# Small products of the tensor engine ordered as lists, and shape changes priced in the ordering model of a two-block kernel

## The chip, the cores and the metric

The kernel runs on one core of a Trainium2 chip. The metric is the device time of one execution in microseconds (us), and the median of several runs is given. The engines are named as in the profile: PE is the tensor engine, PEld its weight loads, DVE the vector engine, ACT the scalar engine, POOL the GpSimd engine and SP the engine that issues most transfers.

## The reference

Two transformer blocks follow each other, on one sequence of 256 positions and width 1024, all in fp32. Cut to what matters here:

```python
# first block: three mixers, a gate, a feed-forward net
proj = rms_norm(x, g_mix) @ w_in           # q_mla, c_kv, k_rope, q_gla, k_gla, v_gla, ..., gates
o_mla = causal_block_attention(q_full, k_full, v_mla, ...)    # 8 heads of 128 + 64 (rotary)
# a[i,j] = sum_d q[i,d] k[j,d] exp(b[i,d] - b[j,d]), in chunks of 64, 4 heads of 128
og = gla_chunked(qg, kg, vg, log_a)
s_m = einsum('bshd,bmhd->bhsm', q_m, k_m) * MEM_DQK ** -0.5    # 4 heads of 64, 256 memory rows
x = x + (gates * [o_mla, o_gla, o_mem]).sum() @ w_o
x = x + square(relu(rms_norm(x, g_ffn) @ w_up)) @ w_down

# second block: a state space branch and a dilated attention
u_s, z_s, q, k, v, z_a, r_s, r_a = split(rms_norm_2(x, norm_w) @ w_in)
y_s = s5_branch(u_s, ...)     # 64 groups of 16 channels, 64 complex states: h = a h + B u, y = Re(C h) + D u
y_a = dilated_attention(q, k, v)   # 8 heads of 64; window 128 at step 1, 512 at step 4, 2048 at step 16
x = x + (sigmoid(r_s) * (y_s * silu(z_s)) @ w_ssm_out + sigmoid(r_a) * (y_a * silu(z_a)) @ w_attn_out) @ w_o
```

## The kernel before

Nothing in the kernel is issued where it is written. The methods of `Net` (one for each stage: `gla_scores`, `mem_attn`, `mla_attn`, `ssm_quarter`, `ssm_scan`, `heads`, `values`, `dilated` and others) call engines through a `Recorder`, and `Plan.add` notes each call as an operation with its buffers and its dependences. `Plan.latest` gives each operation a priority, by a list schedule that runs backwards from the end. `Plan.order` then runs forwards: it keeps a clock for each engine, takes the operation that can start first, by priority among those that are ready, and adds the operation's price (`Plan.price`, in ns) to that engine's clock. An operation gets its buffer when it is taken, from a pool with a fixed number of slots, `BUFS`: 5 of `wr` (weights as they arrive), 4 each of `wh` and `wl` (their high and low parts), 26 of `k4`, 11 of `k2` and 24 of `sm` (results and small vectors), 8 of `ps` (PSUM banks). `Plan.emit` issues the operations in the order found. So each engine's queue is fixed when the program is built, by the prices; on the chip each engine works its queue off in that order and waits wherever an input is not there. All instructions have the line of the emission, L535.

The large products take fp32 weights in two parts: ACT casts `wr` to `wh`, DVE subtracts `wl <- wr, wh`, and PE makes three products for each pair of tiles. They carry some 90% of PE's time.

The change is about the small products, plain fp32, each of which takes two passes of PE in the trace:

- `gla_scores`: per level of the chunked decay 8 products of 64 or 4 x 8 products of 32 rows and columns, then a masked copy on DVE.
- `mem_attn`: 2 pairs of heads; a product is 64 rows (one head's width, on partitions 0 to 63 or 64 to 127) by 128 columns by 256.
- `mla_attn`: for a pair of heads 4 products over 128 rows, and 4 over the 64 rotary rows, which lie on opposite partition halves for the two heads.
- `ssm_quarter`: 16 products of 64 x 32, for each of four quarters of the state space's channels.
- `ssm_scan`: per quarter X = G U, 16 products of 64 x 64 for the real and as many for the imaginary part; ACT copies X out of PSUM, DVE and POOL run the scan to H; then y = T U + C H, 16 products and 32.
- `dilated`: for a pair of heads b and a tile tt of 128 queries, a score tile per head: one product of 64 rows x 128 columns x 256 ("own", the group with step 1) and four of 64 x 64 ("near", the other groups). `softmax_rows` is a masked reduction on DVE, an exponential on ACT and a scaling on DVE; PE transposes, ACT copies, then 12 products of 128 rows x 64 columns make the outputs.

Each of these is an operation of its own in the plan, so that `order` may put a matrix product of another stage, or a transpose, between any two. The price does not depend on what came before on PE. Between 545 and 645 us the scan runs beside `heads` (products, norms and transposes of queries and keys) and before `values`.

## Time and profile before

| | |
|---|---|
| runs | 875.13, 876.12, 878.0 us (median 876.12) |
| profiled execution | 874.69 us, span from first to last instruction 872.8 us |
| mean granted PE clock | 0.996 |
| busy: PE, PEld, DVE, ACT, POOL | 853.1, 757.7, 631.4, 477.4, 22.6 us |
| DMA | 142.09 MB, mean 163 GB/s |

Times count from the start of the span. A row of the timeline joins instructions that follow each other and are alike; its second number is the time from the first one's start to the last one's end, and since PE's products overlap, the start of the next row, not this end, says when PE went on. "64*128 64x256" is a product of 64 rows by 128 columns of weights with 256 moving columns, and "x4" counts passes. The clock is a share of 2.4 GHz.

### The profile page before, as it was taken

The numbers are of one execution on the slowest core, as the hardware profiler recorded it, in microseconds if no ns is written. First come the engines' busy times: TensorE is split into PE (matmuls) and PEld (weight loads), VectorE is DVE, ScalarE is ACT, GpSimd is POOL, SyncE is SP. The second block draws the span as 40 slices with busy tenths as digits, with TensorE's granted clock in tenths as the row PEclk, the third lists the DMA queues.
The fourth block names the chain that finished last, engine by engine and source line by source line (L and its number), as shares of the span: only waits on it lengthen the run. The fifth ranks groups of instructions, "written<-read, shape, count | busy, mean of one in ns | idle before, by whom it ended". The sixth has DMA issues, their size and how long they took to land.

```text
span 872.8 us, 16700 instructions
## 1 busy us (share of the span) xinstructions
PE 853.1 (98%) x6572; PEld 757.7 (87%) x6572; DVE 631.4 (72%) x1478; ACT 477.4 (55%) x782; POOL 22.6 (3%) x40
## 2 busy tenths in 40 slices
PE   8999899999999999999999989999999999999998
PEld 6998787789999989999999878877779769999996
DVE  6998998896756679945544956949997665653584
ACT  6756867644445567555555574444456563554352
POOL 1000000000000000000000051010000000000000
PEclk9999999999999999999999999999999999999999
DMA  9775442145355665665655546661245413565551
GB/s 326 245 238 160 130 126 72 49 137 182 118 192 187 184 210 190 186 192 183 187 183 187 190 125 215 189 210 50 97 135 172 129 50 116 177 192 191 173 177 63
DMA packets 42638, 142.09 MB, mean 163 GB/s; under 512 B 5888, under 2 KB 7040, under 8 KB 42560
## 3 DMA queue, kind: packets, MB, share of 16 engines
q1 hardware_dynamic: 40944, 137.39, 49.4%
q0 software_dynamic: 1472, 3.61, 1.4%
q8 instruction: 51, 0.84, 0.4%
q14 instruction: 27, 0.22, 0.1%
q10 hardware_dynamic: 144, 0.04, 0.0%
HBM read 138.46 MB, written 2.56 MB: 162 GB/s over the span
## 4 chain that ended last, share of the span: by engine, by line
PE 86%; DVE 7%; ACT 3%; issue 2%; DMA 1%; SPq 0%; DVEq 0%; POOL 0%; ACTq 0%; POOLq 0%
PE ps L535 86%; DVE k L535 5%; ACT k L535 2%; DVE sm L535 1%; DVE wl L535 1%; ACT wh L535 1%; DMA wr<-w_mv 1%; DMA k<-ud 1%; SPq L535 0%; DVE c L535 0%; ACT L535 0%; ACT c L535 0%; DVEq L1804 0%; POOL ud L535 0%; ACTq L535 0%
## 5 line engine op out<-in xcount | busy, mean ns | idle before, releaser
L535 DVE TENSOR_TENSOR wl<-wr,wh 128x1024 fp32r<-128x1024 f32 (+2 forms) x258 | 301.7, 1191 | 162.2 <-ACT wh L535 159.5
L535 ACT CAST wh<-wr 128x1024 fp32r<-128x1024 f32 (+2 forms) x258 | 257.5, 1024 | 231.7 <-PE ps L535 205.0
L535 PE MATMUL ps<-k,wh 128*128 128x256 f32 x2048 | 371.8, 284 | 0.5 <-DVE k L535 0.5
L535 PEld LDWEIGHTS ps<-k,wh 128*128 128x128 f32 x2048 | 320.4, 192 | 3.1 <-issue 1.0
L535 PE MATMUL ps<-wh,k 128*128 128x512 f32 (+2 forms) x1024 | 314.0, 384 | 1.7 <-ACT wh L535 1.4
L535 PE MATMUL ps<-k,wl 128*128 128x256 f32 x1024 | 289.6, 283 | 0.6 <-DVE wl L535 0.6
L535 PEld LDWEIGHTS ps<-wh,k 128*128 128x128 f32 x1024 | 188.8, 188 | 38.4 <-ACT wh L535 2.8
L535 PE MATMUL ps<-wl,k 128*128 128x512 f32 (+2 forms) x512 | 196.8, 385 | 2.3 <-DVE wl L535 2.1
L535 PEld LDWEIGHTS ps<-k,wl 128*128 128x128 f32 x1024 | 196.3, 192 | 1.6 <-DVE wl L535 1.0
L535 PEld LDWEIGHTS ps<-wl,k 128*128 128x128 f32 x512 | 96.4, 188 | 22.3 <-DVE wl L535 5.0
L535 DVE TENSOR_TENSOR k<-k,k 128x512 f32<-128x512 f32 (+8 forms) x192 | 91.7, 499 | 13.5 <-ACT k L535 12.9
L535 PE MATMUL ps<-k,k 64*64 64x64 f32 (+7 forms) x1224 | 85.7, 256 | 2.7 <-ACT k L535 2.2
L535 PEld LDWEIGHTS ps<-k,k 64*64 64x64 f32 (+5 forms) x1224 | 62.3, 142 | 23.7 <-issue 13.5
L535 ACT ACTIVATE k<-ps 128x512 f32<-128x512 f32 (+2 forms) x86 | 44.8, 534 | 54.7 <-PE ps L535 54.6
L535 ACT COPY k<-ps 128x512 f32<-128x512 f32 (+7 forms) x119 | 50.7, 456 | 35.1 <-PE ps L535 34.1
L535 PE MATMUL ps<-c,k 128*128 128x128 f32 (+3 forms) x344 | 57.0, 296 | 7.2 <-DVE k L535 3.9
L535 ACT ACTIVATE k<-k 128x512 f32<-128x512 f32 (+3 forms) x72 | 46.5, 672 | 27.2 <-DVE k L535 25.1
L535 PEld LDWEIGHTS ps<-c,k 128*128 128x128 f32 (+2 forms) x344 | 40.8, 149 | 19.6 <-ACT k L535 7.1
L535 DVE TENSOR_TENSOR k<-k,c 128x64 f32<-128x64 f32 (+7 forms) x176 | 47.7, 317 | 0.1
L535 ACT ACTIVATE k<-ps,c 128x256 f32<-128x256 f32 (+2 forms) x76 | 37.0, 540 | 16.3 <-PE ps L535 16.3
L535 DVE SCALAR_TENSOR_TENSOR k<-k,k 128x256 fp32r<-128x256 f32 (+4 forms) x61 | 32.7, 569 | 11.7 <-ACT k L535 11.4
L535 DVE CUSTOM_DVE_ANT_0 k<-ps,c 128x384 f32<-128x384 f32 (+2 forms) x32 | 14.4, 455 | 10.3 <-PE ps L535 10.2
(74 smaller groups left out, 323.4 us busy)
## 6 DMA issues: line engine op xcount, KB each, us to landing
wr<-w_up SPq DMA_DIRECT2D x32, 512.0 KB, 3.9
wr<-w_down SPq DMA_DIRECT2D x32, 512.0 KB, 4.2
wr<-w_gt SPq DMA_DIRECT2D x24, 512.0 KB, 4.0
wr<-w_o SPq DMA_DIRECT2D x16, 512.0 KB, 4.0
wr<-w_k SPq DMA_DIRECT2D x12, 512.0 KB, 4.0
wr<-w_q SPq DMA_DIRECT2D x12, 512.0 KB, 4.1
wr<-w_v SPq DMA_DIRECT2D x12, 512.0 KB, 4.3
wr<-w_qkg SPq DMA_DIRECT2D x8, 512.0 KB, 3.9
```

Of the source, the lines that this page charges most:

```text
L535: getattr(getattr(tc.nc, op.eng), op.name)(*map(live, op.args), **{k: live(v) for k, v in op.kw.items()})
```

## The change

- A new PE operation, `products`, holds a list of products. It is ordered, priced and emitted as one piece; its dependences are those of all its members. Used for: each level of `gla_scores`, the scores of a pair of heads in `mem_attn`, `mla_attn` (over 128 rows first, then rotary) and `dilated` (both own, then near), the 16 products of `ssm_quarter`, in `ssm_scan` X's real part, X's imaginary part, the U products of y and the H products of y, and the 12 products of a `dilated` output. Within the lists for pairs of heads, the two heads alternate.
- `Plan.tiling` gives a product's tile: rows and columns rounded up to 32, 64 or 128. Where it differs from that of the PE operation before, `order` starts the operation later by `SWITCH` = 90 ns plus columns / 1.2, and so it does inside a list.
- Three prices change: 32 columns and over 32 moving 30 to 38 ns; 128 rows x 64 x 64 from 142 to 112; 128 rows, up to 64 columns, more moving columns: 1.15 ns for each.

The products themselves are the same, 5742 PE instructions before and after; the emission of a list has the line L564 and that of other operations L566. The diff, cut to its core:

```diff
+SWITCH = 90
@@ -197,8 +199,12 @@
-        views = [a for a in (*args, *kw.values()) if isinstance(a, View)]
-        outs = [kw["out"]] if "out" in kw else [args[0]]
+        if name == "products":
+            views = [v for a, _ in args[0] for v in a]
+            outs = [a[0] for a, _ in args[0]]
+        else:
+            views = [a for a in (*args, *kw.values()) if isinstance(a, View)]
+            outs = [kw["out"]] if "out" in kw else [args[0]]
@@ -214,6 +220,7 @@
+        op.mode = tuple(self.tiling(*(args[0][j][0] if name == "products" else args)) for j in (0, -1)) if eng == PE else None
@@ -282,9 +289,24 @@
-    def price(op):
+    def tiling(out, l, r):
+        part = lambda n: 32 if n <= 32 else 64 if n <= 64 else 128
+        return part(l.shape[0]), part(int(np.prod(l.shape[1:])))
+    @classmethod
+    def price(cls, op):
+        if op.name == "products":
+            t, last = 0, None
+            for a, _ in op.args[0]:
+                one = Op()
+                one.name, one.eng, one.args, one.kw = "matmul", PE, a, {}
+                mode = cls.tiling(*a)
+                t += cls.price(one) + (SWITCH + mode[1] / 1.2) * (last not in (None, mode))
+                last = mode
+            return t
@@ -293,9 +315,11 @@
-                return 27 if n == 32 else 30
+                return 27 if n == 32 else 38
-                return 57 if half else 142
+                return 57 if half else 112
+            if cols <= 64 and not half:
+                return 1.15 * n
@@ -457,6 +481,9 @@
+            if op.mode is not None:
+                start += (SWITCH + op.mode[0][1] / 1.2) * (op.mode[0] != mode)
+                mode = op.mode[1]
@@ -532,6 +559,10 @@
+                if op.name == "products":
+                    for a, kw in op.args[0]:
+                        tc.nc.tensor.matmul(*map(live, a), **kw)
+                    continue
@@ -1000,14 +1031,12 @@
-        for e in range(8):
-            nc.tensor.matmul(p[:, e], d[:, e, 0:64], d[:, e, 64:128], start=True, stop=True)
+        once = dict(start=True, stop=True)
+        nc.tensor.products([((p[:, e], d[:, e, 0:64], d[:, e, 64:128]), once) for e in range(8)])
-        for e in range(8):
-            for s in (0, 64):
-                nc.tensor.matmul(p[s:s + 32, e], d[:, e, s:s + 32], d[:, e, s + 32:s + 64], start=True, stop=True)
+        nc.tensor.products([((p[s:s + 32, e], d[:, e, s:s + 32], d[:, e, s + 32:s + 64]), once) for e in range(8) for s in (0, 64)])
@@ -1017,9 +1046,8 @@
-            for e in range(8):
-                for s in range(0, P, 32):
-                    nc.tensor.matmul(p[s:s + 32, e], l[:, e, s:s + 32], r[:, e, s:s + 32], start=True, stop=True)
+            nc.tensor.products([((p[s:s + 32, e], l[:, e, s:s + 32], r[:, e, s:s + 32]), once)
+                                for e in range(8) for s in range(0, P, 32)])
@@ -1089,10 +1117,8 @@
-            for t in range(2):
-                for i, hs in enumerate(HALF):
-                    nc.tensor.matmul(ps[i][:, t * S:(t + 1) * S], qmT[hs, hp, t * P:(t + 1) * P],
-                                     self.kmT[hs, hp], start=True, stop=True)
+            nc.tensor.products([((ps[i][:, t * S:(t + 1) * S], qmT[hs, hp, t * P:(t + 1) * P], self.kmT[hs, hp]),
+                                 dict(start=True, stop=True)) for t in range(2) for i, hs in enumerate(HALF)])
@@ -1148,15 +1174,15 @@
-            for i, p in enumerate(ps):
-                hh = 2 * hp + i
-                nc.tensor.matmul(p[:, 0:P], self.qT[hh][:, 0:P], self.kT[hh][:, 0:P], start=True, stop=False, skip_group_check=True)
-                nc.tensor.matmul(p[:, P:384], self.qT[hh][:, P:], self.kT[hh], start=False, stop=False, skip_group_check=True)
-            for t, ks in enumerate((slice(0, P), slice(P, 384))):
-                for p, hs in zip(ps, HALF):
-                    nc.tensor.matmul(p[:, ks], self.qpT[hs, hp, t * P:(t + 1) * P], self.kpT[hs, 0, 0:P * (t + 1)],
-                                     start=False, stop=True, skip_group_check=True)
+            tiles = (slice(0, P), slice(0, P)), (slice(P, 384), slice(0, S))
+            whole = [((p[:, o], self.qT[2 * hp + i][:, t * P:(t + 1) * P], self.kT[2 * hp + i][:, ks]),
+                      dict(start=t == 0, stop=False, skip_group_check=True))
+                     for i, p in enumerate(ps) for t, (o, ks) in enumerate(tiles)]
+            rotary = [((p[:, o], self.qpT[hs, hp, t * P:(t + 1) * P], self.kpT[hs, 0, ks]),
+                       dict(start=False, stop=True, skip_group_check=True))
+                      for t, (o, ks) in enumerate(tiles) for p, hs in zip(ps, HALF)]
+            nc.tensor.products(whole + rotary)
@@ -1397,13 +1423,10 @@
-        for ri in range(2):
-            for j in range(4):
-                for gh in range(2):
-                    hs = slice(64 * gh, 64 * gh + 64)
-                    nc.tensor.matmul(kp[gh][32 * j:32 * j + 32], bbt[hs, ri, j].rearrange("p q a -> p (q a)"),
-                                     cx[hs, 2 * j:2 * j + 2, ri].rearrange("p a t c -> p a (t c)"),
-                                     start=ri == 0, stop=ri == 1, skip_group_check=True)
+        nc.tensor.products([((kp[gh][32 * j:32 * j + 32], bbt[hs, ri, j].rearrange("p q a -> p (q a)"),
+                              cx[hs, 2 * j:2 * j + 2, ri].rearrange("p a t c -> p a (t c)")),
+                             dict(start=ri == 0, stop=ri == 1, skip_group_check=True))
+                            for ri in range(2) for j in range(4) for gh, hs in enumerate(HALF)])
@@ -1478,9 +1501,8 @@
-            for g in range(8):
-                for hs in halves:
-                    nc.tensor.matmul(xp[ri][hs, g], G[hs, 4 * ri + g // 2, g % 2], U[hs, g], start=True, stop=True)
+            nc.tensor.products([((xp[ri][hs, g], G[hs, 4 * ri + g // 2, g % 2], U[hs, g]), dict(start=True, stop=True))
+                                for g in range(8) for hs in halves])
@@ -1497,12 +1519,11 @@
-        for g in range(8):
-            for hs in halves:
-                nc.tensor.matmul(y[hs, g], U[hs, g], self.T[g % 2][hs, 4 * qd + g // 2], start=True, stop=False, skip_group_check=True)
-            for ri in range(2):
-                for hs in halves:
-                    nc.tensor.matmul(y[hs, g], H[hs, ri, g], Cx[hs, g, ri].rearrange("p t c -> p (t c)"), start=False, stop=ri == 1, skip_group_check=True)
+        each = lambda stop: dict(start=False, stop=stop, skip_group_check=True)
+        nc.tensor.products([((y[hs, g], U[hs, g], self.T[g % 2][hs, 4 * qd + g // 2]), dict(start=g == 0, stop=False, skip_group_check=True))
+                            for g in range(8) for hs in halves])
+        nc.tensor.products([((y[hs, g], H[hs, ri, g], Cx[hs, g, ri].rearrange("p t c -> p (t c)")), each(ri == 1))
+                            for g in range(8) for ri in range(2) for hs in halves])
@@ -1576,16 +1597,16 @@
-                for i, a in enumerate(half):
-                    nc.tensor.matmul(pp[i][:, 0:S], self.q2[0][a, b, tt * P:tt * P + P], self.k2T[0][a, b],
-                                     start=True, stop=False, skip_group_check=True)
+                own = [((pp[i][:, 0:S], self.q2[0][a, b, tt * P:tt * P + P], self.k2T[0][a, b]),
+                        dict(start=True, stop=False, skip_group_check=True)) for i, a in enumerate(half)]
+                near = []
-                        for i, a in enumerate(half):
-                            nc.tensor.matmul(pp[i][half[c], S + 64 * j:S + 64 * j + 64], self.q2[g][a, b, cs], self.k2T[g][a, b, cs],
-                                             start=False, stop=j == 1, skip_group_check=True)
+                        near += [((pp[i][half[c], S + 64 * j:S + 64 * j + 64], self.q2[g][a, b, cs], self.k2T[g][a, b, cs]),
+                                  dict(start=False, stop=j == 1, skip_group_check=True)) for i, a in enumerate(half)]
+                nc.tensor.products(own + near)
@@ -1601,16 +1622,13 @@
-            for kb in range(2):
-                for i in range(2):
-                    d = slice(128 * b + 64 * i, 128 * b + 64 * i + 64)
-                    nc.tensor.matmul(o[half[i]], self.v2[0][:, kb, d], pts[i][0][:, kb], start=kb == 0, stop=False, skip_group_check=True)
-            for tt in range(2):
-                for c in range(2):
-                    for i in range(2):
-                        d = slice(128 * b + 64 * i, 128 * b + 64 * i + 64)
-                        nc.tensor.matmul(o[half[i], tt * P + 64 * c:tt * P + 64 * c + 64], self.v2[1 + c][:, tt, d], pts[i][1][:, tt, half[c]],
-                                         start=False, stop=True, skip_group_check=True)
+            dims = [slice(128 * b + 64 * i, 128 * b + 64 * i + 64) for i in range(2)]
+            own = [((o[half[i]], self.v2[0][:, kb, dims[i]], pts[i][0][:, kb]), dict(start=kb == 0, stop=False, skip_group_check=True))
+                   for kb in range(2) for i in range(2)]
+            near = [((o[half[i], tt * P + 64 * c:tt * P + 64 * c + 64], self.v2[1 + c][:, tt, dims[i]], pts[i][1][:, tt, half[c]]),
+                     dict(start=False, stop=True, skip_group_check=True))
+                    for tt in range(2) for c in range(2) for i in range(2)]
+            nc.tensor.products(own + near)
```

What it moves, at two places. First PE in the dilated attention, before: `ps_1700` and `ps_1701` are score tiles of a pair of heads, `ps_1704` that of a next one; k4_1442 and k4_1563 are queries and keys of the group with step 1, the 64x64 rows the other groups, and the 128x128 rows with c are transposes of probabilities.

```order
L535 MATMUL ps_1700_8382<-k4_1442_7175,k4_1563_7756 128x256
L535 MATMUL ps_1700_8382<-k4_1475_7322,k4_1605_7922 64x64
L535 MATMUL ps_1700_8382<-k4_1519_7553,k4_1623_7989 64x64 x2
L535 MATMUL ps_1700_8382<-k4_1475_7322,k4_1605_7922 64x64
L535 MATMUL ps_1701_8389<-k4_1442_7175,k4_1563_7756 128x256
L535 MATMUL ps_1701_8389<-k4_1475_7322,k4_1605_7922 64x64
L535 MATMUL ps_1701_8389<-k4_1519_7553,k4_1623_7989 64x64 x2
L535 MATMUL ps_1701_8389<-k4_1475_7322,k4_1605_7922 64x64
L535 MATMUL ps_1704_8400<-k4_1442_7175,k4_1563_7756 128x256
L535 MATMUL ps_1705_8402<-c_2_39_232,k2_1687_8352 128x128 x2
L535 MATMUL ps_1707_8408<-c_2_39_232,k2_1687_8352 128x128
```

After, at the like place (`ps_1677` and `ps_1678` are the two heads' tiles for one query tile; wl and wh are weights of `values`):

```order
L564 MATMUL ps_1677_8312<-k4_1477_7324,k4_1600_7893 128x256
L564 MATMUL ps_1678_8314<-k4_1477_7324,k4_1600_7893 128x256
L564 MATMUL ps_1677_8312<-k4_1486_7353,k4_1607_7919 64x64
L564 MATMUL ps_1678_8314<-k4_1486_7353,k4_1607_7919 64x64
L564 MATMUL ps_1677_8312<-k4_1573_7772,k4_1612_7937 64x64
L564 MATMUL ps_1678_8314<-k4_1573_7772,k4_1612_7937 64x64
L564 MATMUL ps_1677_8312<-k4_1573_7772,k4_1612_7937 64x64
L564 MATMUL ps_1678_8314<-k4_1573_7772,k4_1612_7937 64x64
L564 MATMUL ps_1677_8312<-k4_1486_7353,k4_1607_7919 64x64
L564 MATMUL ps_1678_8314<-k4_1486_7353,k4_1607_7919 64x64
L566 MATMUL ps_1666_8258<-wh_1667_8260,k4_1299_6384 128x512
L564 MATMUL ps_1682_8330<-k4_1477_7324,k4_1600_7893 128x256
```

Each head's tile stood by itself, its partner's own product five rows later or, as with `ps_1704`, behind transposes; now the two heads' products alternate in one piece.

Second ACT in the scan, before: `k4_1446` takes the squares of the third head group, `k4_1465` X of the second quarter, `k4_1442` a transposed head result, k2_1461 the scan's y; the rows wh<-wr are casts of weights.

```order
L535 CAST wh_1433_7115<-wr_1415_7001 128x1024
L535 CAST wh_1438_7159<-wr_1419_7023 128x1024
L535 CAST wh_1441_7171<-wr_1427_7086 128x1024
L535 ACTIVATE k4_1442_7175<-ps_1440_7168,c_1_2_95 128x512
L535 ACTIVATE k4_1446_7186<-ps_1381_6867 128x512
L535 ACTIVATE k4_1446_7186<-ps_1384_6882 128x512
L535 ACTIVATE k4_1442_7175<-ps_1445_7181,c_1_2_95 128x512
L535 COPY k2_1461_7265<-ps_1449_7194 128x512
L535 COPY k4_1465_7289<-ps_1418_7014 128x512
L535 COPY k4_1465_7289<-ps_1420_7034 128x512
```

After (`k4_1421` takes the squares of the third head group, `k4_1379` X of the second quarter, `k4_1422` inputs U of a later quarter):

```order
L566 CAST wh_1402_6949<-wr_1378_6865 128x1024
L566 CAST wh_1415_7002<-wr_1381_6874 128x1024
L566 CAST wh_1417_7015<-wr_1383_6885 128x1024
L566 ACTIVATE k4_1421_7048<-ps_1384_6888 128x512
L566 ACTIVATE k4_1421_7048<-ps_1389_6904 128x512
L566 COPY k4_1422_7051<-ps_1326_6608 128x512
L566 COPY k4_1379_6868<-ps_1420_7031 128x512
L566 CAST wh_1426_7073<-wr_1391_6913 128x1024
L566 CAST wh_1431_7090<-wr_1404_6960 128x1024
L566 COPY k4_1422_7051<-ps_1360_6760 128x512
```

The squares and both copies of X stood behind a transposed result and 202 of ACT's casts, counted from the start; now the squares and the second copy of X stand behind 196 casts and the first copy, further ahead and not shown, behind 191, and no transposed result is ahead of them.

## Rows read from the trace of the kernel before

**Rows 1.** Page: busy time of each engine; shares of the chain that ended last.
```profile
PE 853.1 (98%) x6572; PEld 757.7 (87%) x6572; DVE 631.4 (72%) x1478; ACT 477.4 (55%) x782; POOL 22.6 (3%) x40
...
PE 86%; DVE 7%; ACT 3%; issue 2%; DMA 1%; SPq 0%; DVEq 0%; POOL 0%; ACTq 0%; POOLq 0%
```

**Rows 2.** Windows: stretch, its length, busy us (instructions) by engine, PE clock, DMA.
```profile
40.00:174.50 134.50, 131.64 (x1158) 109.00 (x1158) 124.04 (x467) 92.39 (x186) 0.00 (x0) 1.00 0.42 131
95.00:114.20 19.20, 16.40 (x100) 13.21 (x98) 19.20 (x44) 16.07 (x25) 0.00 (x0) 1.00 0.37 104
584.60:596.60 12.00, 8.96 (x149) 7.96 (x147) 7.61 (x21) 5.04 (x8) 0.00 (x0) 0.86 0.45 148
596.60:634.00 37.40, 36.12 (x382) 28.49 (x378) 37.40 (x78) 17.67 (x28) 0.00 (x0) 1.00 0.17 57
685.00:720.70 35.70, 35.70 (x317) 23.37 (x316) 24.42 (x79) 20.21 (x53) 0.00 (x0) 1.00 0.20 60
720.70:868.00 147.30, 147.30 (x1148) 143.73 (x1147) 83.66 (x109) 64.96 (x85) 0.00 (x0) 1.00 0.49 158
```

**Rows 3.** Timeline of PE, scan: start, us, instruction, count [idle before].
```profile
606.38 0.39 PE L535 MATMUL ps<-wl,k 128*128 128x512 f32 x1
606.61 0.39 PE L535 MATMUL ps<-wh,k 128*128 128x512 f32 x1
606.93 0.33 PE L535 MATMUL ps<-k,k 64*64 64x64 f32 x4
...
608.08 1.61 PE L535 MATMUL ps<-k,k 64*64 64x64 f32 x48
```

**Rows 4.** Timeline of PE, memory attention scores, from three windows.
```profile
158.25 1.13 PE L535 MATMUL ps<-k,k 64*128 64x256 f32 x4
...
160.82 0.70 PE L535 MATMUL ps<-k,k 64*128 64x256 f32 x2
...
162.85 1.14 PE L535 MATMUL ps<-k,k 64*128 64x256 f32 x6
```

**Rows 5.** Groups, 634 to 721: DVE and ACT, count, busy us, mean ns, idle before.
```profile
L535 DVE CUSTOM_DVE_ANT_0 k<-ps,c 128x384 f32<-128x384 f32 x16 | 8.8, 557 | 8.2 <-PE ps L535 8.1
L535 DVE TENSOR_SCALAR k<-k,sm 128x384 f32<-128x384 f32 x16 | 6.1, 407 | 0.0
...
L535 ACT ACTIVATE k<-k,sm 128x384 f32<-128x384 f32 x16 | 9.8, 618 | 6.0 <-DVE sm L535 5.9
```

**Rows 6.** Timeline of DVE, last tile of the dilated softmax.
```profile
714.99 0.56 DVE L535 CUSTOM_DVE_ANT_0 k<-ps,c 128x384 f32<-128x384 f32 x1 [0.36 <-PE ps L535]
...
716.78 0.42 DVE L535 TENSOR_SCALAR k<-k,sm 128x384 f32<-128x384 f32 x1
```

**Rows 7.** Timeline of PE, the transposes of that tile.
```profile
717.65 0.55 PE L535 MATMUL ps<-c,k 128*128 128x128 f32 x3
```

**Rows 8.** Waits of DVE, 570.9 to 591: us in total, times, longest.
```profile
DVE wl L535 <- ACT wh L535: 11.5, 4, 4.7
DVE sm L535 <- ACT k L535: 1.2, 1, 1.2
```

**Rows 9.** Windows before and after DVE takes up the scan, columns as in 2.
```profile
570.90:590.90 20.00, 17.14 (x164) 14.22 (x159) 7.26 (x6) 8.50 (x12) 2.91 (x4) 1.00 0.70 227
590.90:638.10 47.20, 44.94 (x527) 36.01 (x528) 46.66 (x108) 23.04 (x39) 0.00 (x0) 0.96 0.18 60
```

**Rows 10.** Timeline of ACT, scan: squares of a head group, copies of X.
```profile
589.81 1.08 ACT L535 ACTIVATE k<-ps 128x512 f32<-128x512 f32 x2 [0.75 <-PE ps L535]
...
595.91 2.17 ACT L535 COPY k<-ps 128x512 f32<-128x512 f32 x5 [4.43 <-PE ps L535]
```

**Rows 11.** Timeline of PE, scan: two waits.
```profile
589.12 0.66 PE L535 MATMUL ps<-c,k 128*128 128x128 f32 x4 [1.29 <-ACT k L535]
591.52 5.28 PE L535 MATMUL ps<-k,k 64*64 64x64 f32 x128 [1.75 <-ACT k L535]
```

**Rows 12.** Window after the second wait, columns as in 2 (PE clock).
```profile
592.00:594.00 2.00, 2.00 (x42) 2.00 (x41) 1.69 (x10) 0.00 (x0) 0.00 (x0) 0.50 0.54 197
```

More of the change, by code (lines that the diff above doesn't have):

```diff
@@ L170 @@
 HALF = slice(0, 64), slice(64, P)
+SWITCH = 90
 READ_FIRST = ("copy_predicated",)
 class Op:
-    __slots__ = ("i", "eng", "name", "args", "kw", "outs", "ins", "deps", "cost", "span", "users", "left", "prio", "boost", "bufs", "end", "table", "form")
+    __slots__ = ("i", "eng", "name", "args", "kw", "outs", "ins", "deps", "cost", "span", "users", "left", "prio", "boost", "bufs", "end", "table", "form", "mode")
 class Plan:
@@ L383, in order @@
         ring = dma = 0.0
-        table = 0
+        table, mode = 0, None
         emitted = [False] * N
```

## Prediction

> **What bounds the kernel now.** I read the page first: TensorE (PE) is busy for 98% of the span and its products make 86% of the chain of work that ended last, VectorE (DVE) 7%, ScalarE (ACT) 3% [rows 1]. A busy PE is only one that has a product in flight, so I next read the windows by stage [rows 2], where the reader is to see three regimes. From 95.0 to 114.2 DVE is busy without a gap and PE is not: DVE sets the pace. From 584.6 to 634.0 PE idles 3.04 + 1.28 us, and from 596.6 on DVE has no gap. From 685.0 to 720.7 PE has no gap, DVE is busy 24.4 of 35.7 us, and PE's weight loads 23.4 of 35.7, against 143.7 of 147.3 from 720.7 to 868.0, where plain matrix products run: the dilated attention's small products keep PE occupied without filling it. Last I read the timelines for what one small product costs.
>
> **What the change removes, from two kinds of rows.** *Changes of tile shape.* In the timeline one 128x512 product starts 0.23 us after the one before it (606.38 to 606.61), but a 64x64 product 0.32 us after a 128x512 one (606.61 to 606.93) [rows 3]: a change of shape costs 0.09 us. Counted over the order of instructions, PE changes shape 156 times before and 80 times after: 39 to 19 in the MLA and memory attention (114 to 174), 6 and 6 in the state space setup (499 to 505), 31 to 15 in the scan (505 to 634), 69 to 28 in the dilated attention (634 to 721), 11 and 12 before 114.
>
> *Products on opposite halves of the array.* One score product of 64 rows by 128 columns (two passes) takes 0.70 us, two on the same 64 rows 1.13, and three, of which the first two lie on opposite row halves, 1.14 [rows 4]. So a product on the other half runs beside its neighbour, and the second of a pair is worth 0.43 us. Before, the ordering model nearly always set one head's product apart from its partner's; the lists put both heads' side by side, in the dilated scores for 8 pairs where there was none, in MLA for 4 pairs (0.43 + 0.21 us each), in the memory attention for 3 more than now. A run of such products also carries some 0.1 us to start (0.70 less 0.43 less the 0.09 of leaving is 0.18; I take 0.1).
>
> The Trainium skill says the same of the mechanism and gives no time: "Tiles operate independently", and a change of mode drains the engine (TensorEngine Tiling (Array Packing), Key Properties). Its section PSUM Bottleneck speaks against the change: once TensorE is faster, reading the results out of PSUM may become the bound. That is rival B below.
>
> **Dilated attention.** 41 changes x 0.092 = 3.8, 8 pairs x 0.43 = 3.5, 8 runs fewer x 0.1 = 0.8, and some 20 fragments of 64x64 and 128x64 products that are joined, at about 0.05 each (four passes take 0.26 from 606.93 to the next row's start; 48 in a row take 1.61 [rows 3], so a fragment carries 0.14, of which 0.09 is the change): 1.0. Together 9.1 us of PE work in a stretch where PE is the bound. Against it: two score tiles now come at once. For one tile DVE reduces (557 ns) and scales (407), ACT exponentiates (618) [rows 5]; the last tile of today goes from its reduction at 714.99 over its scaling at 716.78 [rows 6] to its transposes at 717.65 [rows 7], 2.7 us. A pair's second tile waits one more reduction, so 3.2. In the new order between 2.9 and 3.8 us of PE work (sums of row durations as above) lies between a group's last scores and their transposes. Waits of 0 to 1.5 us in each of the four groups follow, 0 to 6; I take 2.0, nearer to nothing since DVE and ACT have a third of their time free there. Net **-7.1**, bounds -9.1 and -3.
>
> **The scan (505 to 634).** 16 changes x 0.092 = 1.5. The larger part is a side effect on ACT's queue. From 570.9 to 590.9 DVE does 7.26 us of work and waits 11.5 us for ACT's weight casts and 1.2 for its squares [rows 8]; then its work of the scan stands in a row, 46.66 us of 47.20 until the last scan products come at 638 [rows 9]. ACT idles before its copies of X, which release that work, until 595.91, and does the third head group's squares only at 589.81 [rows 10]: they stand in its order behind casts and a transposed result that wait for PE. In the new order no transposed result is ahead of them and six casts fewer (eleven for the first copy of X). DVE could then start the scan's work 20 us sooner and be through at about 571 + 7.3 + 46.7 = 625; PE, by its new order and these durations, comes for the last of it at about 624. So the waits of today go (1.29 at 589.12 and 1.75 at 591.52 [rows 11], more in small pieces: 4.3 by [rows 2], and 1.4 for the half clock, granted 0.50 (1.2 GHz) from 592 to 594 after those waits [rows 12], where 128 passes take 5.28 us, against 1.61 for 48 at full clock [rows 3]), 5.7 in all, and a new one of one to four takes part of it back. I take 3.0; bounds 5.7 gained and, if DVE is late as today, the loss of rival C. Net **-4.5**.
>
> **First block (40 to 175).** PE work falls by 20 changes x 0.092 = 1.8, 3 pairs x 0.43 = 1.3, MLA 4 x 0.64 = 2.6, and 7 runs x 0.1 = 0.7: 6.4 us. But over 40 to 175 DVE works 124.0 of 134.5 us and PE loses only 2.9 by idling [rows 2], and the linear attention's levels are now all taken earlier, whole, so that DVE gets their masked copies sooner and what it does for MLA later. Following DVE's work in order, its tightest place moves from 105 us (1.3 us in hand) to some 140 us, where PE would now be 2.3 us ahead of it: 3.6 of the 6.4 go into waits at once, and I allow 0.9 for gaps that DVE keeps. Net **-1.9**, bounds -6.4 and +1.5 (the present idle of 2.9 grown by half).
>
> **Setup and weights' streams.** The setup's products (499 to 505) keep their count of changes, and whatever their new order saves lies ahead of a norm in which PE waits for DVE and ACT: nothing. The lists add no instruction on any engine, five copies move between ACT and DVE (some 0.5 us each, off the path), and the streams of weights keep their order; from 721 on both orders are the same and PE-bound (147.30 of 147.30 busy [rows 2]).
>
> **The sum.** -7.1 - 4.5 - 1.9 = -13.5 us on the span of 872.8: 859.3. The profiled run took 874.69, 1.9 more than its span, and the median of the runs shown, 876.12, lies 1.4 above that run: 859.3 + 1.9 + 1.4 = **862.6**.
>
> **Rivals.** *B: the softmax chain takes PE's place.* The waits in the dilated stretch eat most of its 9.1 us, nothing comes through in the first block and the scan gives 2.5: -2 - 0 - 2.5, about 871.6. For it: two tiles at once, and little but dilated work left in PE's order for those 20 us, where 16 reductions and scalings alone keep DVE 15 us and the exponentials ACT 10. Against it: DVE is idle 32% of 685 to 720.7 now, and waits there for PE. *C: slower.* The scan's last products now stand together behind 96 products of the head group (22 us), with less of other work between them. If DVE again waits some 12.7 us between 571 and 591 (no free buffer for X's or the squares' results, or ACT held by casts), it is through at 638 while PE is there at 624: 14 us of waits, 1 to 2 more by the half clock that follows such waits, against 7.1 + 1.5 + 1.9 gained: 881 or so. It decides from about 9 us of DVE idle in that stretch. Against it: both orders keep the same buffer counts, and the last six of the casts that stood ahead of the copies stand behind them now. *D: everything comes through.* -9.1 - 7.2 - 6.4, about 853. It needs a DVE that is never late; its 100% from 95 to 114 speaks against. *E: the change doesn't do what it says*, as halves don't overlap in these lists or the shapes' price is hidden by weight loads: changes alone on the bound stretch give 3.8, about 872; [rows 3, 4] speak against it directly.
>
> **How the numbers follow.** Forecast (857 to 868) 0.50, B 0.22, D 0.13, E 0.07, C 0.08. Within 0.3% of 876.1, about the least a measurement of this kernel can tell, is 873.5 to 878.7. Faster: the forecast, D, and most of B and E, 0.86; within 0.3%: 0.06; slower: C, 0.08. The range leaves out C, the slowest of B and the fastest of D: 854 to 872.
>
> **What would show it.** Right: the dilated stretch from its first scores to its last output shrinks by 6 us or more, and PE's passes of a pair's 64x128 products start within 0.01 us of each other by halves; DVE's gap around 571 to 591 is below 5 us; PE idles 1 to 4 us before the last scan products. Wrong: lone rows of two 64x128 passes; PE idle of over 4 us before the dilated transposes; a granted clock of half between 600 and 640; DVE idle over 9 us in the scan.

## The result, and the profile after

| | before | after |
|---|---|---|
| median of four runs | 877.06 us (875.13 to 878.63) | 848.31 us (847.4 to 848.93) |
| ratio | | 0.9672, 95% interval 0.9648 to 0.9696 |
| profiled execution, span | 874.69, 872.8 us | 847.4, 845.5 us |
| busy: PE, DVE, ACT | 853.1, 631.4, 477.4 us | 826.7, 626.4, 478.9 us |

The forecast was 862.6 with a range of 854.0 to 872.0: the direction was right and the mechanisms it names showed, but the size was half of what came (13.5 of 27.3 us of the span). By stage, from the starts of PE's products in the two traces (a stage's time is the sum, over its products, of the time from one start to the next):

| stretch | gained | forecast |
|---|---|---|
| first block, to the linear attention's output gate | 6.4 | 1.9 |
| state space setup and norm | 1.7 | 0 |
| scan with the heads of queries and keys | 8.4 | 4.5 |
| values and dilated attention | 10.8 | 7.1 |
| span | 27.3 | 13.5 |

The page after, busy times and the chain that ended last (before: [rows 1]). PE works 26.4 us less for the same products, DVE's part in the chain grows from 7% to 11%:

```profile
PE 826.7 (98%) x6572; PEld 746.0 (88%) x6572; DVE 626.4 (74%) x1473; ACT 478.9 (57%) x787; POOL 22.8 (3%) x40
...
PE 83%; DVE 11%; issue 2%; ACT 2%; DMA 1%; DVEq 0%; SPq 0%; ACTq 0%
```

Windows of after: from 40 us to the end of the attentions, the scan to the last head product, the dilated stretch (columns as in [rows 2]):

```profile
40.00:167.48 127.48, 124.35 (x1156) 106.56 (x1155) 126.04 (x497) 92.72 (x186) 0.00 (x0) 1.00 0.44 140
502.60:625.50 122.90, 118.40 (x1187) 103.24 (x1186) 106.77 (x236) 65.71 (x102) 14.74 (x24) 1.00 0.51 160
625.50:693.30 67.80, 65.12 (x549) 53.16 (x547) 48.29 (x108) 45.86 (x94) 0.00 (x0) 1.00 0.42 133
```

The two later stretches in the kernel before:

```profile
512.20:651.50 139.30, 133.16 (x1225) 111.49 (x1224) 110.20 (x238) 66.44 (x101) 11.81 (x19) 0.99 0.46 141
651.50:720.20 68.70, 68.70 (x508) 52.66 (x506) 46.95 (x108) 42.67 (x86) 0.00 (x0) 1.00 0.40 127
```

To be seen: up to the attentions' end DVE is now busy 126.0 of 127.5 us, where it was 124.0 of 134.5 [rows 2], and PE idles 3.1 us, as before (2.9). The scan's stretch shrinks by 16.4 us and PE's idle time in it from 6.1 to 4.5, of which 1.47 is the norm's wait at 504.33 (shown below). The dilated stretch hardly shrinks, since the ordering has put more of the matrix products into it; what counts there is its products. PE's timeline, first list of a later pair, then two waits:

```profile
672.99 1.09 PE L564 MATMUL ps<-k,k 64*128 64x256 f32 x20
674.02 0.77 PE L566 MATMUL ps<-c,k 128*128 128x128 f32 x5
674.71 2.57 PE L564 MATMUL ps<-k,k 64*128 64x256 f32 x44
678.70 0.41 PE L566 MATMUL ps<-c,k 128*128 128x128 f32 x2 [1.42 <-DVE k L566]
...
689.13 1.20 PE L566 MATMUL ps<-c,k 128*128 128x128 f32 x9 [1.26 <-DVE k L566]
```

The 20 passes at 672.99 are a list: two own products of 64x128 and eight of 64x64. It takes 1.03 us from its start to the next. Before, one own product alone was 0.70 us [rows 4]. The transposes at 678.70 and 689.13 wait 1.42 and 1.26 us for the softmax on DVE, 2.7 in all; nothing waited there before.

In the scan, ACT's squares and its copy of X after, and all that DVE waited for between 550 and 600:

```profile
562.92 1.07 ACT L566 ACTIVATE k<-ps 128x512 f32<-128x512 f32 x2
563.88 1.19 ACT L566 COPY k<-ps 128x512 f32<-128x512 f32 x2
```

```profile
DVE wl L566 <- ACT wh L566: 0.6, 1, 0.6
```

The squares stood at 589.81 before, the copies of X at 595.91 [rows 10], and DVE waited 12.7 us [rows 8]; now 0.6. PE has one wait left ahead of a head group's transposes, of the size that was forecast:

```profile
618.43 0.52 PE L566 MATMUL ps<-c,k 128*128 128x128 f32 x3 [1.86 <-ACT k L566]
```

At the norm ahead of the second block's products, after and, in the second fence, before:

```profile
500.68 2.18 PE L566 MATMUL ps<-c,k 128*128 128x128 f32 x16 [0.53 <-ACT k L566]
504.33 0.48 PE L566 MATMUL ps<-k,wh 128*128 128x256 f32 x2 [1.47 <-DVE k L566]
```

```profile
509.02 3.62 PE L535 MATMUL ps<-c,k 128*128 128x128 f32 x16 [3.22 <-DVE k L535]
```

Before, PE waited 3.22 us in one piece and the 16 transposes behind it took 3.62 us; now the waits are spread and the 16 take 2.18. The windows of that place, before and then after (the granted clock stands behind POOL's column), show the price of the one long wait:

```profile
509.00:511.00 2.00, 1.98 (x10) 1.83 (x11) 0.54 (x1) 1.93 (x6) 1.80 (x4) 0.52 0.18 39
511.00:513.00 2.00, 1.82 (x9) 1.47 (x7) 0.25 (x1) 1.95 (x7) 2.00 (x4) 0.63 0.63 133
```

```profile
500.50:503.00 2.50, 2.18 (x16) 1.71 (x16) 0.09 (x1) 2.42 (x8) 1.22 (x2) 1.00 0.12 43
```

In the two windows behind the wait the granted clock averages 0.52 and 0.63, that is, some 3.4 of the 4 us at half; now it stays at 1.00.

### The profile page after: what moved, and what is told of

It is laid out like the page before. It is cut to its first block, busy times and chain, and to the rows that moved or that the text cites. A ratio compares the mean times of both kernels' runs of the same rounds, so it can differ in the third digit from the quotient of the medians.

```text
span 845.5 us, 16706 instructions
## 1 busy us (share of the span) xinstructions
PE 826.7 (98%) x6572; PEld 746.0 (88%) x6572; DVE 626.4 (74%) x1473; ACT 478.9 (57%) x787; POOL 22.8 (3%) x40
## 4 chain that ended last, share of the span: by engine, by line
PE 83%; DVE 11%; issue 2%; ACT 2%; DMA 1%; DVEq 0%; SPq 0%; ACTq 0%
PE ps L566 81%; DVE k L566 7%; PE ps L564 3%; DVE wl L566 2%; ACT k L566 2%; DVE sm L566 2%; DMA wr<-w_mv 1%; ACT wh L566 0%; DMA c<-gains 0%; DVEq L1822 0%; SPq L566 0%; DVEq L566 0%; DVE c L566 0%; ACTq L566 0%
## 5 line engine op out<-in xcount | busy, mean ns | idle before, releaser
L566 DVE TENSOR_TENSOR wl<-wr,wh 128x1024 fp32r<-128x1024 f32 (+2 forms) x258 | 301.5, 1192 | 153.3 <-ACT wh L566 150.7
L566 ACT CAST wh<-wr 128x1024 fp32r<-128x1024 f32 (+2 forms) x258 | 257.8, 1024 | 218.5 <-PE ps L566 195.9
L566 PE MATMUL ps<-k,wh 128*128 128x256 f32 x2048 | 372.3, 284 | 1.5 <-DVE k L566 1.5
L566 PEld LDWEIGHTS ps<-k,wh 128*128 128x128 f32 x2048 | 320.6, 192 | 4.0 <-ACT k L566 1.7
L566 PE MATMUL ps<-wh,k 128*128 128x512 f32 (+2 forms) x1024 | 311.3, 383 | 1.4 <-ACT wh L566 1.4
L566 PE MATMUL ps<-k,wl 128*128 128x256 f32 x1024 | 289.9, 283 | 0.6 <-DVE wl L566 0.6
L566 PEld LDWEIGHTS ps<-wh,k 128*128 128x128 f32 x1024 | 189.2, 188 | 38.0 <-ACT wh L566 2.3
L566 PEld LDWEIGHTS ps<-k,wl 128*128 128x128 f32 x1024 | 196.4, 192 | 1.7 <-DVE wl L566 1.1
L566 PE MATMUL ps<-wl,k 128*128 128x512 f32 (+2 forms) x512 | 195.5, 383 | 0.7 <-DVE wl L566 0.7
L566 PEld LDWEIGHTS ps<-wl,k 128*128 128x128 f32 x512 | 96.2, 188 | 20.0 <-DVE wl L566 2.3
L566 DVE TENSOR_TENSOR k<-k,k 128x512 f32<-128x512 f32 (+8 forms) x192 | 91.9, 503 | 13.6 <-ACT k L566 13.1
L566 ACT ACTIVATE k<-ps 128x512 f32<-128x512 f32 (+1 forms) x86 | 44.4, 531 | 51.7 <-PE ps L566 51.6
L566 ACT COPY k<-ps 128x512 f32<-128x512 f32 (+7 forms) x123 | 52.0, 452 | 23.2 <-PE ps L564 12.3
L566 ACT ACTIVATE k<-k 128x256 fp32r<-128x256 f32 (+3 forms) x73 | 47.0, 668 | 27.6 <-DVE k L566 22.1
L566 PE MATMUL ps<-c,k 128*128 128x128 f32 (+2 forms) x312 | 45.2, 281 | 7.6 <-DVE k L566 3.9
L566 DVE TENSOR_TENSOR k<-k,c 128x64 f32<-128x64 f32 (+7 forms) x176 | 47.6, 320 | 0.1
L564 PE MATMUL ps<-k,k 64*64 64x64 f32 (+7 forms) x1136 | 46.8, 242 | 0.5 <-DMA k<-ud 0.2
L566 PEld LDWEIGHTS ps<-c,k 128*128 128x128 f32 (+2 forms) x312 | 35.0, 142 | 13.7 <-ACT k L566 5.0
L564 PEld LDWEIGHTS ps<-k,k 64*64 64x64 f32 (+5 forms) x1136 | 37.1, 134 | 10.0 <-issue 4.7
L566 ACT ACTIVATE k<-ps,c 128x256 f32<-128x256 f32 (+2 forms) x76 | 36.0, 538 | 15.5 <-PE ps L566 15.5
L566 DVE SCALAR_TENSOR_TENSOR k<-k,k 128x256 fp32r<-128x256 f32 (+4 forms) x61 | 32.8, 569 | 14.9 <-ACT k L566 14.3
L566 ACT ACTIVATE k<-k,sm 128x384 f32<-128x384 f32 (+2 forms) x32 | 16.9, 530 | 8.1 <-DVE sm L566 8.1
```

Source lines behind the costliest of these rows:

```text
L564: tc.nc.tensor.matmul(*map(live, a), **kw)
L566: getattr(getattr(tc.nc, op.eng), op.name)(*map(live, op.args), **{k: live(v) for k, v in op.kw.items()})
```

## The experiments

Each kernel was timed beside the kernel before on the same chip. The last two columns are from its profiled run: the end of the first block (start of its last product), and from there to the last product of all.

| kernel | median, us | ratio to before (95%) | first block | second |
|---|---|---|---|---|
| before | 876.2 to 877.1 | 1 | 498.5 | 370.2 |
| changed | 848.31 | 0.9672 (0.9648 to 0.9696) | 492.2 | 349.3 |
| e1 X and squares behind | 861.48 | 0.9831 (0.9812 to 0.985) | 494.1 | 361.2 |
| e2 before, X and squares early | 865.92 | 0.9873 (0.9854 to 0.9892) | 499.7 | 361.7 |
| e3 prices only | 869.09 | 0.9918 (0.99 to 0.9936) | 496.8 | 366.2 |
| e4 lists only | 853.76 | 0.9738 (0.9721 to 0.9754) | 502.5 | 346.2 |
| e5 heads apart in the lists | 854.06 | 0.9737 (0.9712 to 0.9762) | 494.8 | 355.3 |
| e6 prices, dilated lists | 856.51 | 0.9764 (0.9745 to 0.9783) | 496.8 | 353.5 |
| e7 prices, first block's lists | 862.92 | 0.9833 (0.9811 to 0.9855) | 494.2 | 366.8 |
| e8 all but linear attention's lists | 856.69 | 0.9766 (0.9745 to 0.9788) | 500.8 | 350.4 |
| e9 all but MLA's and memory's lists | 861.72 | 0.9837 (0.9817 to 0.9858) | 501.3 | 349.3 |
| e10 all but the scan's lists | 851.40 | 0.971 (0.9684 to 0.9736) | 491.7 | 352.9 |
| e11 charge in the first block only | 844.83 | 0.9646 (0.9624 to 0.9668) | 492.3 | 346.2 |
| e12 changed, again | 848.87 | 0.9688 (0.967 to 0.9707) | 494.5 | 349.2 |

The profiled run need not lie at the median: that of e7 took 867.12 us, 4.2 above its median, and that of e9 856.36, 5.4 below.

Theory 1 was that the scan was held up by ACT's order, theory 2 that the lists themselves shorten it.

**e1, the changed kernel with the old order of four ACT instructions.**

```diff
+        for b in self.behind["then"]:
+            a = self.behind["first"][0]
+            ops[a].users.append(b)
+            ops[b].left += 1
```

> The changed kernel with all its lists and prices, but the ordering is told that ACT's squares of the third head group and its copies of X of the second quarter follow the first transposed head result, as they did before; ACT's order there is then row for row that of the kernel before (202 casts ahead), PE changes shape 86 times instead of 80. Theory 1 (ACT's order of these four instructions was what held the scan up): DVE again waits 10 us or more for casts in the scan, PE waits and falls to the half clock, and the time is 6 to 8 us above the changed kernel, 854 to 856. Theory 2 (the lists themselves shorten the scan, ACT's order came along by chance): 848 to 850.

861.48, 13 us slower than the changed kernel and more than theory 1 asked for. DVE's waits from 565 to 592, two rows of ACT, two of PE, and a window with the clock:

```profile
DVE wl L571 <- ACT wh L571: 11.9, 3, 6.7
DVE sm L571 <- ACT k L571: 1.2, 1, 1.2
```

```profile
585.65 1.09 ACT L571 ACTIVATE k<-ps 128x512 f32<-128x512 f32 x2 [0.74 <-PE ps L571]
...
592.10 2.23 ACT L571 COPY k<-ps 128x512 f32<-128x512 f32 x5 [4.79 <-PE ps L569]
```

```profile
584.96 0.66 PE L571 MATMUL ps<-c,k 128*128 128x128 f32 x4 [1.29 <-ACT k L571]
...
587.36 5.70 PE L569 MATMUL ps<-k,k 64*64 64x64 f32 x128 [1.75 <-ACT k L571]
```

```profile
589.00:592.00 3.00, 3.00 (x62) 3.00 (x60) 2.65 (x11) 0.00 (x0) 0.00 (x0) 0.50 0.07 27
```

It is the picture of before, lists and all: DVE waits 13.1 us, the squares run at 585.65, PE waits 1.29 and 1.75 us, and at 589 to 592 the granted clock is 0.50. Not all of the 13 us are ACT's four instructions: PE's order moved with them, it changes shape six times more, and it waits 2.45 us at 576.4 for a transfer of the scan's input, where the changed kernel waits 0.22. Theory 2 falls with e2 and e10, which move the lists and ACT's order one at a time.

**e2, the kernel before with those ACT instructions early.**

```diff
+            self.plan.boost = 30000
             nc.any.copy(X[:, ri], xp[ri])
+            self.plan.boost = None
```

The same two lines stand around the squares of the heads.

> The kernel before, no lists and no price of a shape change, with a higher priority in the forward ordering for two kinds of ACT instructions of the second block: the squares of the heads and the copies of X. ACT's order in the scan is then that of the changed kernel (196 casts ahead of the squares); PE changes shape 133 times, 23 less than before. Theory 1: the scan's waits go, 5 to 6.5 us, and 23 changes x 0.09 = 2.1 us: 868 to 870. Theory 2: only the changes pay: 874 to 875.

865.92, 10.3 us faster than before without any list. DVE's waits from 560 to 600:

```profile
DVE sm L535 <- ACT k L535: 1.2, 2, 0.7
DVE wl L535 <- ACT wh L535: 0.9, 1, 0.9
```

12.7 us have become 2.1. Its second block is 8.5 us shorter; the 23 shape changes less are 2.1 of that, so the order is worth 6.4 here (the profiled run is 1.6 above the median; by the medians it is 8.2), and up to 12 in e1, by the second block.

**e3, prices without lists.** The products are issued one by one again, for instance in the scan (the like in every function of the change):

```diff
-            nc.tensor.products([((xp[ri][hs, g], G[hs, 4 * ri + g // 2, g % 2], U[hs, g]), dict(start=True, stop=True))
-                                for g in range(8) for hs in halves])
+            for g in range(8):
+                for hs in halves:
+                    nc.tensor.matmul(xp[ri][hs, g], G[hs, 4 * ri + g // 2, g % 2], U[hs, g], start=True, stop=True)
```

> The kernel before with the price of a shape change and the three new prices, but no lists: PE changes shape 122 times, 34 less than before, no pair of heads stands side by side more often than before, and ACT's order in the scan is that of the changed kernel. Theory 1: 3.1 us for the changes and 5 to 6.5 for the scan: 867 to 869. Theory 2: 873.

869.09, at the edge of theory 1's interval; the second block gains only 4.0, less than e2's with the same ACT order. PE waits 2.59 us at 580.61 for the scan's input, with half clock behind it, and windows of the dilated stretch show what took another part back:

```profile
676.00:680.00 4.00, 4.00 (x34) 2.28 (x33) 2.54 (x7) 1.42 (x4) 0.00 (x0) 1.00 0.62 223
680.00:682.00 2.00, 2.00 (x12) 1.23 (x11) 1.74 (x9) 0.82 (x3) 0.00 (x0) 0.50 0.00 0
682.00:684.00 2.00, 2.00 (x6) 1.52 (x6) 1.22 (x4) 0.84 (x3) 0.00 (x0) 0.50 0.00 0
684.00:686.00 2.00, 2.00 (x8) 1.60 (x7) 1.17 (x1) 0.80 (x1) 0.00 (x0) 0.50 0.00 0
...
688.00:690.00 2.00, 2.00 (x21) 1.25 (x21) 0.91 (x3) 1.06 (x3) 0.00 (x0) 1.00 0.34 129
```

From 680 the clock is granted at 0.50, though PE has no gap there or in the 4 us before; two runs of the same ten passes show it:

```profile
678.24 1.07 PE L566 MATMUL ps<-k,k 64*128 64x256 f32 x10
...
679.68 1.57 PE L566 MATMUL ps<-k,k 64*128 64x256 f32 x10
```

1.07 us, then 1.57. All four runs of e3 have a mean clock of 0.990 to 0.992, those of the changed kernel 0.997 to 1.0 (0.994 to 0.998 in e12).

**e4, lists without prices.**

```diff
-SWITCH = 90
+SWITCH = 0
```

The three new prices go too.

> The changed kernel with all lists, but the prices of before and no charge for a shape change, in the ordering or inside a list: 79 changes, the same pairs, ACT's order in the scan that of the changed kernel. If the lists carry the gain: within 2 us of the changed kernel, 846 to 850. If the ordering needs to know the price of a change: 855 or more.

853.76, between the two: the second block is 3 us shorter than with the prices, the first 10 us longer. In that first block PE waits up to 3.71 us at a time (at 149.39, for DVE) and is granted half the clock for some 13.7 us.

**e5, lists emitted head by head.**

```diff
-                    for a, kw in op.args[0]:
+                    for a, kw in first + sorted(rest, key=lambda m: seen.index(m[0][0].buf)):
```

> The changed kernel with the same plan, only that each list for a pair of heads is emitted head by head (in the dilated scores one head's own product and its four near ones, then the partner's; in MLA and the memory attention one head's 64-row products, then the other's). No instruction leaves its list. PE's runs of 64x128 products go from 14 to 22 and its shape changes from 80 to 96. If opposite halves really overlap: 8 runs x 0.63 us = 5.0, and some 8 more changes x 0.09 = 0.7 not in them, in the dilated stretch, PE the bound there but for about 3 us of waits that shrink by part of it: 4 to 6 above the changed kernel, 852 to 854. If only the uninterrupted lists count and the alternation of heads does not: 16 x 0.09 = 1.5, 849.8.

854.06, 5.7 us slower. The same list as above, and the row behind it:

```profile
678.65 2.08 PE L575 MATMUL ps<-k,k 64*128 64x256 f32 x20
680.66 0.77 PE L577 MATMUL ps<-c,k 128*128 128x128 f32 x5
```

2.01 us from start to start against 1.03. Of 8 x 0.98 = 7.8 us some 2.7 vanish in the softmax waits, which are gone here; the dilated products with their waits take 27.7 us instead of 22.8. The alternation, not the list alone, is worth that. The 0.98 holds two changes of shape.

**e6, e7: prices with the dilated lists, or with the first block's lists** (the other functions as in e3).

> The kernel before with the new prices and the lists of the dilated attention alone (scores and outputs): 93 shape changes, 8 pairs of heads side by side. If the dilated lists are worth what the two traces show for that stretch, 9.5 us less the part that the prices alone give (about 2): 7 to 8 below the kernel with the prices alone. If its gain hangs on the other lists (PE arriving with DVE less loaded): 4 or less.

> The kernel before with the new prices and the lists of the first block alone (linear attention, memory attention, MLA): 107 shape changes. The first block of the changed kernel ends 6.4 us earlier. If DVE's pace had bound it as the prediction said, 2 below the kernel with the prices alone; if DVE's gaps close because PE comes sooner, 5 to 6.5 below it.

e6 is 12.6 us below e3, not 7 to 8, and all of it in the second block: the pairs, the changes, and the clock, which does not fall in its dilated stretch (the dilated products take 22.8 us with their waits, in e3 33.1). e7 is 6.2 below, as forecast if DVE's gaps close, but they don't: DVE is busy 129.3 of 132.4 us up to the attentions' end in e3 and 126.2 of 129.5 in e7, 3.1 and 3.4 us of gaps. The windows, e3 and then e7:

```profile
40.00:172.38 132.38, 131.49 (x1158) 109.61 (x1157) 129.28 (x510) 93.23 (x188) 0.00 (x0) 1.00 0.42 133
```

```profile
40.00:169.54 129.54, 127.23 (x1156) 109.05 (x1155) 126.17 (x497) 92.46 (x186) 0.00 (x0) 0.97 0.42 137
```

e7's first block shows only 2.6 of that in the profiled runs, but e7's profiled run lies 4.2 above its median, with the clock at half for some 6.8 us from 81.4, which no wait of PE precedes.

**e8, e9, e10: one group of lists left out.**

> The changed kernel without the lists of the linear attention's levels: 84 shape changes. If whole levels, taken early, are what took away PE's waits on the weights and on MLA's keys in the first block (about 4 us): 851 to 853. If the pairs of heads in MLA and memory attention give the first block's gain: 848 to 849.5.

> The changed kernel without the lists of MLA and the memory attention (their heads set apart again, 20 runs of 64x128 products instead of 14, 91 shape changes); the linear attention's levels stay whole. If the whole levels, by giving DVE its masked copies early, carry the first block's gain: the first block ends within 2 us of the changed kernel's, 848 to 851 in all. If the pairs carry it: 853 to 856.

> The changed kernel without the lists of the state space scan (X and y issued product by product again). ACT's order of the squares and of X's copies in the scan stays that of the changed kernel. If that order and not the lists shortens the scan: 1 to 2 us above the changed kernel for the shape changes, 849 to 851. If the scan's lists are needed: 854 or more.

e8 and e9 miss all that was expected: without the linear attention's lists, or without MLA's and the memory's, the first block ends later than in the kernel before. One window of e8, and the same of the changed kernel:

```profile
120.00:140.00 20.00, 12.83 (x351) 11.19 (x349) 20.00 (x69) 11.27 (x19) 0.00 (x0) 0.89 0.56 184
```

```profile
120.00:140.00 20.00, 19.06 (x370) 16.36 (x369) 19.62 (x82) 12.57 (x30) 0.00 (x0) 1.00 0.33 105
```

In e8 DVE has no gap and PE idles 7.2 of 20 us, most of it in one wait for DVE, so DVE's queue holds PE up by the order of its work, not by gaps:

```profile
140.14 1.94 PE L566 MATMUL ps<-c,k 128*128 128x128 f32 x8 [6.41 <-DVE sm L566]
```

e10 is 2.5 us slower than e12, the changed kernel beside it, and just outside what theory 1 gave; its squares run at 562.82, as in the changed kernel. But the loss is not the price of shape changes, as was expected: PE changes shape 80 times in e10's trace, as often as in the changed kernel. What its trace has instead is a wait for a transfer of the scan's input, and half clock in the products behind it; e10, then the changed kernel:

```profile
574.48 2.93 PE L566 MATMUL ps<-k,k 64*64 64x64 f32 x64 [3.06 <-DMA k<-ud]
```

```profile
575.52 2.08 PE L564 MATMUL ps<-k,k 64*64 64x64 f32 x64 [0.22 <-DMA k<-ud]
```

e3, e6 and e7 wait 2.1 to 3.1 us there too, and so does e1 (2.45), which has the scan's lists: it is the order that decides it, not the lists as such.

**e11, charge and new prices in the first block alone; e12, the changed kernel again.**

```diff
-            if op.mode is not None:
+            if op.mode is not None and i < self.mark:
```

The prices of `products` and the three new ones hold up to the same mark, the first operation of the second block.

> The changed kernel with the charge and the new prices in the first block alone; in the second block the lists are ordered by the prices of before. PE's order is that of the changed kernel to the end of the first block and that of the kernel with lists alone (e4) from then on. If the two blocks do not touch each other: the first block ends as in the changed kernel and the second takes what it took in e4, 3 us less: 844 to 847.

> The changed kernel itself, beside the others on the same chip: 847.5 to 849.5.

844.83 against 848.87: faster than both kernels, and as forecast. The two blocks' orders can be chosen apart. The second block's 3 us are mostly the softmax waits: in the dilated stretch of e11, as in that of e4, PE waits 0.2 us, where the changed kernel waits 2.7. e12 also shows how much the same order varies: its first block ends 2.3 us later than in the other profile of the changed kernel (at 127.05 PE waits 1.89 us instead of 0.94 and is granted half the clock for some 3.4 us), the second takes the same time.

## Why the prediction was wrong in size

**Changes of shape**: 156 became 80, and the price of 0.09 us holds in the trace after, where one product starts 0.12 us behind another of its shape (562.95 to 563.07) and the first of a new shape 0.21 (563.07 to 563.28):

```profile
562.95 0.28 PE L566 MATMUL ps<-k,wl 128*128 128x256 f32 x1
563.07 0.28 PE L566 MATMUL ps<-k,wh 128*128 128x256 f32 x1
563.28 1.15 PE L564 MATMUL ps<-k,k 64*64 64x64 f32 x32
```

Their sum is shown by no run by itself: e3 has 34 changes fewer, but another order and clock as well.

**Opposite halves**: the mechanism held (e5), and one term was sized too small. I let the pair's own products overlap and gave the near ones only a fragment's 0.05. A list takes 1.03 us; its own pair is 0.63 of that by [rows 4] (0.70 less the part that lies under the next product), so eight near products of two heads take 0.40, about what four of one head took. Alternation saves 0.98 per pair, two changes of shape (0.18) included, where I had 0.43 + 0.1 + 0.18 and some fragments: the step that failed is the 0.05 for each fragment. The dilated products fell by 9.5 us with the new waits in them, 12.2 without; I had 9.1. The waits themselves, 2.7, were forecast as 2.0, and rival B, which gave them most of the gain, is refuted by them. Rival E falls with e5. The Trainium skill's warning on it (TensorEngine Tiling (Array Packing), PSUM Bottleneck), that copying results out of PSUM may become the bottleneck, is given for a 4x speed-up of TensorE; here the waits for the softmax, whose first step reads PSUM, took back 2.7 of the 12.2 us, and 0.2 in the orders of e4 and e11.

**The scan**: the mechanism was the one named, and the step that failed is "I take 3.0". I took the present waits from two windows (584.6 to 634.0), where the stretch from 512 to 651 holds 6.1 us of idle PE and e1 and e2 put the order's worth at 12 and 6.4. By the windows, as an estimate: of the 8.4 us gained, PE's idle time gives 3.1 (6.1 to 4.5, less the norm's 1.47) and the half clock up to 1.7 (some 3.4 us from 591.0 before, none now): 4.8 where I took 3.0. With 1.5 for the changes of shape some 2.1 are left, which lie in products that follow each other sooner without a wait; no run takes them apart. The wait that was to take part of it back came (1.86 at 618.43). Windows show idle time alone: of e1's 12 us, 7.4 are PE's idle time, up to 1.7 the half clock behind the wait, and 0.6 by the price above six changes of shape more; the rest I can't place. Rival C, DVE waiting for ACT as long as before, is what e1 builds, with 13.1 us of waiting: its price of 14 to 16 was near the 12 measured, its sign wrong, since the rest gained more than I allowed.

**First block**: the step that failed is "3.6 of the 6.4 go into waits at once, and I allow 0.9". I added the new waits to the present ones. In the trace they took their place: PE's idle time went from 2.9 to 3.1, and the 6.4 us of PE work came through whole, because DVE's 10.5 us of gaps closed to 1.4. In e12, the same kernel, the gaps are 4.0 (DVE busy 125.74 of 129.76 us), PE idles 4.2, and 4.0 us come through. DVE's pace was read rightly as the bound, but its gaps were not a part of the pace. That it is no law shows in e4, e8 and e9: other orders of nearly the same work end 8 to 10 us later, with PE waits of 3.71, 6.41 and 2.84 us in one piece. Nor are gaps that close the whole of it: the prices alone (e3) already leave only 3.1 us of them, and e7's lists gain with 3.4. Which of the ordering's choices decides that stays open.

**Setup and norm**: forecast as nothing, since PE waits there; but PE's wait of 3.22 us had also cost clock behind it (0.52 and 0.63), and the part gained 1.7 with the waits spread, most of it in the 16 transposes (3.62 us before, 2.18 now).

Of the cases, D (everything comes through, 853, chance 0.13) was nearest; the span fell 4.6 us more than in D (1.7 in values and dilated attention, 1.7 in the setup, 1.2 in the scan), and my range ended above the result.

## What to carry to other kernels

When an order is made by a list scheduler, a change to a few prices or pieces reshuffles queues that it does not name: compare the order of every engine that some other engine waits for, and test the suspicious difference by itself on the old kernel (e2), where it may pay without the change. Small products that use half of the array's rows or columns should alternate between halves in one uninterrupted run, all of them, not just the largest. And when the bound engine's feeder has gaps, count them as room that an order may use (the changed kernel) or lose (e4, e8, e9), until a row shows what fills them.

## What was not expected of the hardware

Eight 64x64 products, each of two passes, from two heads and both column halves take 0.40 us beside the 0.38 of four from one head: 25 ns a pass on average. The Trainium skill (TensorE: Matmul & The Clock Gate, in "Wait — 56ns, not 53.3ns?") gives a floor of about 25 ns from start to start, however small the product. Between products on different tiles the trace goes below it, and the measurement decides: within the list the passes of opposite halves start 7 ns apart, and 46 passes of 128 rows by 32 columns in the linear attention take 0.61 us from the first start to the last end, 13 ns each:

```profile
126.30 0.61 PE L564 MATMUL ps<-k 128*32 128x32 f32 x46 [0.94 <-issue]
```

The granted clock of PE fell to half (1.2 GHz) in e3 from 680 to 686 without any idle PE before it, in a run of small products and shape changes in which weight loads were busy 2.28 of 4 us; the kernel before ran a like mix from 685 to 720.7 at full clock [rows 2], so what decides it is not known from here. It was no single case: the clock fell so in the dilated stretch of e2 (at 689.7) and of e7 (678.8 and 702.6), and in the first block of e5 and e7 at about 82, where PE has no wait either.
